# A trunk layer on one core: the second norm applied to rows ahead of the transposes, one plain half in place of three in the up projection, and the rounded blocks of w_down made inside the up projection

## The chip, the cores and the metric

The kernel runs on one core of a Trainium2 chip. The metric is the device time of one execution in microseconds (us). Matmuls run on TensorE (PE; PEld is its weight load), element work on VectorE (DVE) and ScalarE (ACT), and GpSimd (POOL) and SyncE (SP) mostly issue DMAs: SP the loads and stores, POOL those that add what they read to what lies at the destination. Each engine goes through its own instructions in the order in which they stand.

## The reference

One layer on 512 tokens of width 2048, all in float32, with a feed-forward width F of 5632:

```python
h = rms_norm(x, pre_mix_g)
# q, k, v, u from h @ w_in; chunked attention -> a; pooling of u -> p
m = concat([a, p]) @ w_o
x = x + rms_norm(m, post_mix_g)
h = rms_norm(x, pre_ffn_g)
up = causal_dwconv(h @ w_up, conv_w, conv_b)          # 3 taps along the tokens
y = (gelu(up[..., :F]) * up[..., F:]) @ w_down
x = x + rms_norm(y, post_ffn_g)
```

`rms_norm(x, g)` is x times one over the root of the row's mean square, times g per column.

## The kernel before, in words

**Numbers.** A matmul takes a float32 operand as two parts: hi, the value rounded by ACT, and lo, the rest, which DVE subtracts (`split`). A plain product sums three matmuls, hi x hi, hi x lo and lo x hi (`mm3`, L162 to L165). The products of the up projection carry the lo parts of h side by side with the hi parts in one 512-wide operand, so they take one wide matmul (L170) and one narrow one (L176) for each of 8 blocks of 128 rows (`mm2`).

**w_o.** The product with w_o is made from seven products of half size (the scheme of Strassen and Winograd) in the order 1, 2, 5, 3, 6, 7, 4, each in two column halves cc; `wo_product(i, cc)` takes four weight tiles q, and after each may call a function `between(q)`. The rows of x are in four tiles of 128 tokens: the first half is tiles 0 and 1, the second tiles 2 and 3. When y of a half is complete, its squares (L910, ACT), the norm (L952 to L955, with a power on POOL at L954), and x2 = x + y*r*gain (L967, DVE) follow. `keep_x` squares x2 for the next norm and stores x2 (L974; the second half to x2d in DRAM).

**Transposes.** `turn_back(t0, pair, ps)` transposes x2, not normed, for two blocks of 128 columns, by PE (L981), and splits the result out of PSUM with the gain of the next norm (L143 on ACT, L144 on DVE) into hT, the tiles gT0 to gT3. The eight pairs of the first half stand inside products (7,1) and (4,0); those of the second half come after w_o.

**Ready blocks.** The down projection also is made of seven products. For some of its block sums, SP's copies and POOL's adds in DRAM (`sums_in_dram`, copy L304, add L308, one step at each call of `more_sums`) make the sums t40, t41 and others. Six other parts are loaded, split and stored as hi and lo while w_o runs: `ready_blocks`, one step after each weight tile of a w_o product.

**Up projection.** F is cut in 22 blocks u of 256 columns, each with a gate (p = 0) and a value (p = 1): 44 halves. Three are plain (PLAIN = 3): 16 blocks of rows x 2 column blocks x `mm3`. The gate of u = 0 is made in two parts of 256 tokens (`gate_part`), its first part ahead of and between the transposes of the second half. The other 41 halves are made by seven products each, of sums of quarters of h (hs: h5, h3, h6, and the difference of quarters in hT) and of sums of blocks of w_up. The class `Factors` holds the order of all products (pairs (k, i): half k, product i), loads the raw blocks (SP, `raw4` and `raw_x` rings), adds the second block to them by a POOL DMA (L1362, `add`), and splits them into the `w4` ring (`make`); `prefetch(n)` keeps `make` four products and the loads ten ahead. `seven` issues a product, `keep` takes it from PSUM, `keep_all` puts a half together and multiplies it by RR. h here is not normed: R, one over the root of the mean square per token, is spread over partitions by a matmul (L223) and multiplied into every half afterwards (L1243 for plain ones).

After that follow the taps, the gelu, the product, which goes to gd in DRAM, and the down projection.

**What sets the order.** PE's order is written by hand; the other engines' rows stand as their producers and consumers are called, with `issue_after` at some places. A row's semaphore waits hold all that stands behind it on its engine.

Of the kernel before, what the change touches and what calls it, by code (L numbers as in the profile page):

```python
# [30 lines left out]
PLAIN = 3  # L31
CU = 4
AHEAD = 3
SCALE = 1.0 / math.sqrt(DH)
# [47 lines left out]
def encoder_layer(ctx: ExitStack, tc: tile.TileContext, x, xT, vecs, rel, post_mix, post_ffn,  # L82
# [427 lines left out]
    weights.limit = len(specs)  # L510
# [102 lines left out]
    with tc.tile_pool(name="p1", bufs=2, reuse_waits="tile") as p1:  # L613
# [225 lines left out]
        def ready_blocks():  # L839
            for at, j in ready_parts:  # L840
                v, hi = (p2.tile([P, 1024], dt, tag=tag, name=tag) for tag, dt in (("rw", F32), ("rwh", F32R)))
                lo = v.bitcast(F32R)
                nc.sync.dma_start(v.rearrange("p (a b) -> p a b", a=2),
                                  first_block(at[0], at[1] - 1, 0)[:, 2 * j:2 * j + 2, :])
                for _ in range(4):
                    yield
                split(hi, lo, v)
                yield
                for dest, part_ in zip(ready_w[at], (hi, lo)):
                    nc.sync.dma_start(dest[:, 2 * j:2 * j + 2, :], f32(part_).rearrange("p (a b) -> p a b", a=2))  # L850
                for _ in range(3):
                    yield

        ready_steps = ready_blocks()

# [3 lines left out]
        def wo_product(i, cc, left, between=None):  # L859
            at = 2 * cc + (4 if i in (2, 5, 3) else 0)  # L860
            ps = wo_banks[at:at + 2]
            for q in range(4):
# [6 lines left out]
                if i != 1:  # L869
                    next(ready_steps, None)  # L870
# [12 lines left out]
    with tc.tile_pool(name="p2", bufs=1, reuse_waits="tile") as p2:  # L883
        def rows2(name):

            return p2.tile([P, 2, D // 2], F32, tag=name, name=name)

        y11, y12, y21, y22 = (rows2(f"y{n}") for n in (11, 12, 21, 22))
        gain = p2.tile([P, D], F32, name="gain")
        nc.sync.dma_start(gain, post_mix[None, :].to_broadcast([P, D]))  # L890
        small = p2.tile([P, 64], F32, name="small")
        ssq = small[:, :16].rearrange("p (a b) -> p a b", a=NT)
        ssq2, rm = (small[:, i:i + 8].rearrange("p (a b) -> p a b", a=NT) for i in (16, 24))
        total = small[:, 32:36]
        nc.vector.memset(ssq, 0.0)

# [11 lines left out]
        def square(v, total):  # L908
            junk = p2.tile([P, D // 2], F32, tag="junk", name="junk")
            nc.scalar.activation(junk[:, :v.shape[-1]], v, AF.Square, accum_out=total)  # L910
# [64 lines left out]

        def turn_back(t0, pair, ps):

            for k in range(2):
                kb = 2 * pair + k
                for t in range(2):  # L980
                    nc.tensor.transpose(ps[:, k * T + t * P:k * T + (t + 1) * P],  # L981
                                        xn[t0 + t][:, kb * P:(kb + 1) * P], ident)
# [72 lines left out]
        rstd(rt, total)  # L1055

    mixing.close()

# [683 lines left out]
```

## Time and profile before

| what | us or share |
|---|---|
| runs | 1860.69, 1864.02, 1864.48 (median 1864.02) |
| profiled execution | 1858.89, span 1857.1 |
| PE busy | 1842.6 (99%) |
| DVE busy | 1532.2 (83%) |
| ACT busy | 1084.4 (58%) |
| POOL busy | 302.8 (16%) |
| mean granted clock of TensorE | 0.999 |

Busy time is the union of an engine's instructions; the rest of the span it waits. A row of the timeline gives start, length, engine, line, operation, output from input; "x8" is eight such in a row, and brackets tell how long the engine stood idle before it and what released it.

### The profile page before, as it was taken

What the parts mean: (1) busy time and instruction counts of PE and PEld (TensorE: products, weight loads), DVE (VectorE), ACT (ScalarE), POOL (GpSimd) and SP (SyncE); (2) the same over time, 40 slices, a digit from 0 to 9 for tenths busy, and PEclk for the clock granted to TensorE, in tenths of its full rate; (3) what the DMA queues carried; (4) which work ended last, traced back from release to release, by engine and by line L of the source; (5) the groups of instructions that cost most, each with busy time, mean ns of one, the idle gap of its engine ahead of it and who ended that gap; (6) DMA issues with size and microseconds to landing.
All of it is one profiled execution on the core that took longest, in us unless ns stands there. A gap on an engine that the chain in (4) does not pass through costs nothing.

```text
span 1857.1 us, 25452 instructions
## 1 busy us (share of the span) xinstructions
PE 1842.6 (99%) x9598; PEld 1584.3 (85%) x9598; DVE 1532.2 (83%) x1799; ACT 1084.4 (58%) x1376; POOL 302.8 (16%) x402
## 2 busy tenths in 40 slices
PE   9999999999999999999999999999999999999998
PEld 7888888888879888888888888888888888888886
DVE  6988778878588988888887888888887899899876
ACT  7654455456564666566565665666655655565553
POOL 3411001100000112212122122121121001111101
PEclk9999999999999999999999999999999999999999
DMA  8599977998987798888888988889888977777785
GB/s 319 171 319 302 322 230 233 267 264 310 326 308 202 185 220 195 205 204 200 201 200 203 207 202 195 204 206 205 199 179 288 363 224 171 193 211 178 176 230 157
DMA packets 139338, 426.01 MB, mean 229 GB/s; under 512 B 11920, under 2 KB 15376, under 8 KB 133520
## 3 DMA queue, kind: packets, MB, share of 16 engines
q0 software_dynamic: 54864, 173.56, 45.8%
q1 hardware_dynamic: 84352, 250.84, 38.8%
q8 instruction: 75, 1.23, 0.3%
q14 instruction: 47, 0.39, 0.1%
HBM read 370.35 MB, written 104.33 MB: 256 GB/s over the span
## 4 chain that ended last, share of the span: by engine, by line
PE 69%; DMA 1%; DVE 1%; issue 0%; ACT 0%; DVEq 0%; POOLq 0%; ACTq 0%
PE qa L170 16%; PE qa L176 8%; PE qg L170 8%; PE qg L176 4%; PE qd L170 4%; PE pa L162 4%; PE pa L165 4%; PE pa L164 4%; PE qd L176 2%; PE pg L162 2%; PE pg L165 2%; PE pg L164 2%; PE up L165 1%; PE up L162 1%; PE up L164 1%; PE pd L164 1%
## 5 line engine op out<-in xcount | busy, mean ns | idle before, releaser
L140 ACT ACTIVATE wfh<-wx 128x1024 fp32r<-128x1024 f32 x192 | 203.4, 1059 | 154.3 <-PE qg L170 54.4
L170 PE MATMUL qa<-gT,wfh 128*128 128x512 f32 x1152 | 288.6, 392 | 0.0
L141 DVE TENSOR_TENSOR wfl<-wx,wfh 128x1024 fp32r<-128x1024 f32 x192 | 234.6, 1222 | 61.0 <-ACT wfh L140 44.0
L170 PEld LDWEIGHTS qa<-gT,wfh 128*128 128x128 f32 x1152 | 207.2, 189 | 37.1
L1362 POOL DMA_DIRECT2D wx<-in_w_up x122 | 104.6, 858 | 502.6 <-DVE wfl L141 467.9
L140 ACT ACTIVATE wfh<-wy 128x1024 fp32r<-128x1024 f32 x96 | 101.7, 1060 | 108.5 <-PE qg L170 57.2
L170 PE MATMUL qg<-h,wfh 128*128 128x512 f32 x656 | 162.2, 389 | 0.1
L176 PE MATMUL qa<-gT,wfl 128*128 128x256 f32 x1152 | 161.4, 283 | 0.6 <-ACT zm L1422 0.6
L176 PEld LDWEIGHTS qa<-gT,wfl 128*128 128x128 f32 x1152 | 151.5, 191 | 4.9 <-ACT zm L1422 0.8
L170 PEld LDWEIGHTS qg<-h,wfh 128*128 128x128 f32 x656 | 122.9, 188 | 25.9 <-ACT zb L1418 0.5
L141 DVE TENSOR_TENSOR bl<-b,bh 128x2048 fp32r<-128x2048 f32 x56 | 127.2, 2285 | 19.1 <-ACT bh L140 11.7
L140 ACT ACTIVATE bh<-b 128x2048 fp32r<-128x2048 f32 x56 | 106.0, 1911 | 52.8 <-DVE b L1126 21.8
L141 DVE TENSOR_TENSOR wfl<-wy,wfh 128x1024 fp32r<-128x1024 f32 x96 | 117.1, 1220 | 12.6 <-ACT wfh L140 7.8
L162 PE MATMUL pa<-bh,ah 128*128 128x512 f32 x320 | 124.5, 389 | 0.0
L164 PE MATMUL pa<-bl,ah 128*128 128x512 f32 x320 | 124.5, 389 | 0.0
L165 PE MATMUL pa<-bh,al 128*128 128x512 f32 x320 | 124.5, 389 | 0.0
L141 DVE TENSOR_TENSOR wfl<-wz,wfh 128x1024 fp32r<-128x1024 f32 x48 | 58.7, 1223 | 54.2 <-PE qa L170 54.2
L176 PEld LDWEIGHTS qg<-h,wfl 128*128 128x128 f32 x656 | 89.5, 190 | 6.4
L170 PE MATMUL qd<-gT,wfh 128*128 128x512 f32 x384 | 94.9, 389 | 0.0
L176 PE MATMUL qg<-h,wfl 128*128 128x256 f32 x656 | 91.5, 282 | 0.0
L170 PEld LDWEIGHTS qd<-gT,wfh 128*128 128x128 f32 x384 | 71.9, 188 | 14.9
L170 PE MATMUL qa<-h,wfh 128*128 128x512 f32 x328 | 82.1, 392 | 0.0
(554 smaller groups left out, 4352.5 us busy)
## 6 DMA issues: line engine op xcount, KB each, us to landing
wx<-in_w_up POOLq DMA_DIRECT2D x122, 512.0 KB, 6.2
b<-in_w_down SPq DMA_DIRECT2D x32, 1024.0 KB, 7.0
wt<-in_w_o POOLq DMA_DIRECT2D x24, 1024.0 KB, 16.8
wx<-in_w_up SPq DMA_DIRECT2D x43, 512.0 KB, 5.5
wz<-in_w_up SPq DMA_DIRECT2D x41, 512.0 KB, 5.7
wy<-in_w_up SPq DMA_DIRECT2D x41, 512.0 KB, 4.7
wy<-in_w_up POOLq DMA_DIRECT2D x41, 512.0 KB, 6.7
sum<-part POOLq DMA_DIRECT2D x38, 512.0 KB, 6.4
```

Of the source, the lines that this page charges most:

```text
L140: rounded = nc.scalar.activation(hi, src, AF.Copy)
L141: rest = nc.vector.tensor_sub(lo, src, f32(hi))
L162: nc.tensor.matmul(ps, l[0], r[0], start=first, stop=False, skip_group_check=onto)
L164: nc.tensor.matmul(low, l[0], r[1], start=False, stop=False, skip_group_check=onto)
L165: nc.tensor.matmul(ps, l[1], r[0], start=False, stop=last, skip_group_check=onto)
L170: nc.tensor.matmul(ps, w[0][:, kb], pairs[kb][0], start=fresh and not kb, stop=last, skip_group_check=not fresh)
L176: nc.tensor.matmul(ps[:, sl], w[1][:, kb], pair[:, sl], start=False, stop=last, skip_group_check=not fresh)
L1362: nc.gpsimd.dma_start(self.raw[k, what], self.block(k, m, kh), accum_op=ALU.add)
```

## The change

h of the second half is normed as rows before it is transposed: the same factor that R brought is now multiplied into x2 ahead of the transposes (ACT for tiles 0 and 1, DVE for tiles 2 and 3). The transposes' results are kept whole in `wholes` (ACT's copy with the gain), and splits and h sums read these; the multiplications by R and RR go. The transposes of the first half all stand in product (4,0), two pairs for each weight tile. One half is plain, with its gate in full width; the others are by seven products. The products begin in another order, five of them ahead of the transposes of the second half, and their blocks are prefetched from product (4,1) of w_o on. The ready blocks leave w_o and go into the order of the products, at every 24th place from the 60th.

```diff
-PLAIN = 3
+PLAIN = 1
+READY_FROM, READY_EVERY = 60, 24
...
-        ready_steps = ready_blocks()
...
-                if i != 1:
-                    next(ready_steps, None)
...
+        def norm_x(t0):
+            r = rn[:, t0:t0 + 2]
+            nc.vector.reduce_sum(r, ssq2[:, t0:t0 + 2, :], axis=AX.X)
+            nc.vector.tensor_scalar(r, r, 1.0 / D, EPS, op0=ALU.mult, op1=ALU.add)
+            nc.gpsimd.tensor_tensor(r, r, mhalf[:, :2], op=ALU.pow)
...
         def turn_back(t0, pair, ps):
...
-                                        xn[t0 + t][:, kb * P:(kb + 1) * P], ident)
+                                        hn[t0 + t][:, kb * P:(kb + 1) * P], ident)
...
-                turn_back.last = split(*g_half(hT, kb, t0 // 2), ps[:, k * T:(k + 1) * T], col(V_PREFFN, kb))
+                nc.scalar.activation(v[:, kb % 8, :], ps[:, k * T:(k + 1) * T], AF.Copy, scale=col(V_PREFFN, kb))
+            if pair % 2:
+                i = pair // 2 % 2
+                split(*quarter(pair // 4, t0 // 2, i), v[:, 4 * i:4 * i + 4, :])
...
-        finish_last(0, wo_product(4, 0, a22, first_half(4)))
-        ps4 = wo_product(4, 1, a22)
+        finish_last(0, wo_product(4, 0, a22, first_half))
...
+                self.alone, self.open = (0, 1, 2, 3, n - 1), False
...
-                begin = [(0, 1), (0, 2), (0, 5), (1, 1), (0, 3)]
+                begin = [(k, i) for k in range(3) for i in (1, 2)] + [(0, 5), (3, 1), (0, 3), (3, 2), (0, 6)]
...
+                self.order[6:6] = [("w", q) for q in range(4)]
+                for at in range(len(ready_parts)):
+                    self.order.insert(READY_FROM + READY_EVERY * at, (None, at))
...
+                if k is None:
+                    at, j = ready_parts[i]
+                    parts = w4("rwh"), w4("rwl")
+                    split(*parts, self.raw[k, i])
+                    for dest, v in zip(ready_w[at], parts):
+                        nc.sync.dma_start(dest[:, 2 * j:2 * j + 2, :], f32(v).rearrange("p (a b) -> p a b", a=2))
...
+        ps4 = wo_product(4, 1, a22, lambda q: factors.prefetch(q + 1))
         finish_last(1, ps4)
         norm(2)
...
+        x2(2, y21, 0, whole)
+        x2(2, y22, 1, whole)
+        keep_x(2)
+        norm_x(2)
+        for t in range(2, 4):
+            hn[t] = acc8(f"hn{t}", "A")
+        for l in range(2):
+            cs = slice(l * D // 2, (l + 1) * D // 2)
+            for t in range(2, 4):
+                nc.vector.tensor_scalar_mul(hn[t][:, cs], xn[t][:, cs], rn[:, t:t + 1])
...
-            nc.vector.tensor_mul(flat(z), flat(z), flat(RR))
...
+        for k, i in factors.order[:5]:
+            start(k, i)
+        for pair in range(4):
+            turn_back(2, pair, bank(f"xt{pair}"))
+            more_sums(1)
+        start(2, 2)
+        for pair in (4, 5):
+            turn_back(2, pair, bank(f"xt{pair}"))
+        factors.open = True
+        ups = [bank(f"up0_{j}") for j in range(2)]
+        for q in range(4):
+            if q == 1:
+                for pair in (6, 7):
+                    turn_back(2, pair, bank(f"xt{pair}"))
...
+            w = weights.get(f"w00_{q}", 0)
...
+        h_sums()
+        gates[0] = gate(0, plain_z(ups))
```

In the new source most of these lines stand one or more lines further down (L308 becomes L309, L304 becomes L305, L140 and L141 become L141 and L142; L1362 becomes L1087).

POOL's queue after w_o, before: t40 and t41 are sums of w_down blocks, small holds the norm's numbers (L954 is the power of a norm), rt is R's row, and wx the first block that a product of the up projection takes as a sum.

```order
L954 TENSOR_TENSOR small_4123<-small_4123,mhalf_82 128x2 [waits DVE_49,PE_49,Activation_49]
L308 DMA t40_114<-in_w_down 512x1x512 [waits DMAHW0_49]
L954 TENSOR_TENSOR small_4123<-small_4123,mhalf_82 128x2 [waits DVE_49]
L308 DMA t41_115<-in_w_down 512x1x512 [waits DMAHW2_49]
L218 TENSOR_TENSOR rt_117<-rt_117,mhalf_82 128x4 [waits DVE_49,Activation_49]
L1362 DMA wx_5725<-in_w_up 128x1024 [waits DMAHW5_49,DMAHW4_49,DMAHW6_49,DMAHW3_49,DMAHW7_49,DMAHW1_49,DVE_49]
```

The same place after: L971 is the power of the row norm, and wx_5430 the block of product (0,5).

```order
L944 TENSOR_TENSOR small_4130<-small_4130,mhalf_82 128x2 [waits DVE_49]
L309 DMA t40_114<-in_w_down 512x1x512 [waits DMAHW2_49]
L971 TENSOR_TENSOR small_4130<-small_4130,mhalf_82 128x2 [waits DVE_49]
L309 DMA t41_115<-in_w_down 512x1x512 [waits DMAHW5_49]
L1087 DMA wx_5430<-in_w_up 128x1024 [waits DMAHW4_49,DMAHW3_49,DMAHW6_49,DMAHW1_49,DMAHW7_49,DMAHW0_49,Activation_49]
```

t40's add now stands behind the norm of y and ahead of the row norm's power, and the first block sum directly behind t41's add.

SP's queue at the same place, before: w00 to w01 are plain weights, x2d the stores of x2.

```order
L152 DMA w10_1r_5177<-in_w_up 128x2x512 [waits DMAHW1_49,DVE_49]
L304 DMA t40_114<-t60_112 16x16384 [waits DMAHW0_49,DMASW2_49]
L152 DMA w10_2r_5384<-in_w_up 128x2x512 [waits DMAHW3_49,DVE_49]
L304 DMA t41_115<-t61_113 16x16384 [waits DMAHW2_49,DMASW3_49]
L152 DMA w10_3r_5435<-in_w_up 128x2x512 [waits DMAHW4_49,DVE_49]
L152 DMA w01_0r_5486<-in_w_up 128x2x512 [waits DMAHW5_49,DVE_49]
L974 DMA x2d2_4112<-x2_5205 128x2048 [waits DVE_49]
L974 DMA x2d3_4113<-x3_5207 128x2048 [waits DMAHW6_49,DVE_49]
```

And after:

```order
L153 DMA w00_3r_5180<-in_w_up 128x2x512 [waits DMAHW4_49,DVE_49]
L305 DMA t40_114<-t60_112 16x16384 [waits DMASW2_49]
L964 DMA x2d2_4112<-x2_4968 128x2048 [waits DMAHW3_49,DVE_49]
L964 DMA x2d3_4113<-x3_5100 128x2048 [waits DVE_49]
L305 DMA t41_115<-t61_113 16x16384 [waits DMAHW5_49,DMASW3_49]
L1062 DMA wx_5430<-in_w_up 128x1024 [waits DMAHW6_49,DVE_49]
L1062 DMA wx_5433<-in_w_up 128x1024 [waits DMAHW7_49,DVE_49]
```

t41's copy moved from ahead of the x2d stores to behind them, and the load of wx_5430 is behind both.

ACT's queue where the last transposes of the second half are evacuated, before (xt30 and xt31 are the last banks of transposes):

```order
L140 ACTIVATE w10_1h_5437<-w10_1r_5177 128x1024 [waits DMAHW7_49,PE_49]
L143 ACTIVATE gT3_4809<-xt30_5443,vec_69 128x256 [waits PE_49]
L143 ACTIVATE gT3_4809<-xt31_5452,vec_69 128x256 [waits PE_49]
L143 ACTIVATE gT3_4809<-xt30_5443,vec_69 128x256 [waits DVE_49]
L143 ACTIVATE gT3_4809<-xt31_5452,vec_69 128x256 [waits DVE_49]
```

And after (a21 and a22 are `wholes` of the second half, h50 an h sum, wfh the rounded block of a product):

```order
L141 ACTIVATE gT2_4788<-a22_5220 128x4x256 [waits Activation_49]
L141 ACTIVATE wfh_5442<-wx_5430 128x1024 [waits DMASW6_49,DVE_49,PE_49]
L989 ACTIVATE a22_5220<-xt6_5471,vec_69 128x256 [waits PE_49]
L989 ACTIVATE a22_5220<-xt6_5471,vec_69 128x256
L989 ACTIVATE a22_5220<-xt7_5478,vec_69 128x256 [waits PE_49]
L989 ACTIVATE a22_5220<-xt7_5478,vec_69 128x256
L141 ACTIVATE h50_5575<-a22_5220 128x4x256 [waits DVE_49]
L141 ACTIVATE gT3_4789<-a22_5220 128x4x256 [waits Activation_49]
```

The rounding of the block that POOL's add completes (DMASW6) now stands ahead of the last evacuations; before, no block sum was read until the plain halves were through.

More of the change, by code (lines that the diff above doesn't have):

```diff
@@ L1017, in encoder_layer @@
+        factors = Factors()
+        ps4 = wo_product(4, 1, a22, lambda q: factors.prefetch(q + 1))
         finish_last(1, ps4)
         norm(2)
[L1021 to L1029 removed]
@@ L1466, in encoder_layer @@
             next(r)
-        end = factors.alone[-1]
         def next_first():
```

384 lines of the change are left out of this document (180 added, 204 removed).

## Prediction

> **What bounds the kernel now.** First the page: which engine has no idle time.
>
> ```profile
> span 1857.1 us, 25452 instructions
> PE 1842.6 (99%) x9598; PEld 1584.3 (85%) x9598; DVE 1532.2 (83%) x1799; ACT 1084.4 (58%) x1376; POOL 302.8 (16%) x402
> ```
>
> TensorE is 99% busy, so a change pays by taking matmuls away and costs wherever it makes PE wait. The next view is the same busy time by stretch (columns: stretch, length, PE, PEld, DVE, ACT, POOL, granted clock, DMA share, GB/s); the third is the list of waits from 490 to 660.
>
> ```profile
> 480.00:552.00 72.00, 69.30 (x321) 57.11 (x320) 52.94 (x62) 43.89 (x69) 0.72 (x1) 1.00 0.88 318
> 552.00:622.00 70.00, 70.00 (x420) 62.49 (x419) 59.78 (x77) 35.41 (x52) 6.76 (x6) 1.00 0.67 196
> 622.00:1400.00 778.00, 777.33 (x4464) 686.00 (x4463) 647.54 (x762) 474.95 (x581) 168.08 (x201) 1.00 0.88 202
> PEld m L164 <- DVE wo_1l L141: 3.0, 1, 3.0
> PE m L164 <- DVE wo_1l L141: 2.7, 1, 2.7
> ACT rwh L140 <- DMA rw<-in_w_down: 9.3, 2, 5.8
> ```
>
> PE never waits between 552 and 622, where the plain halves stand, nor to speak of in the up projection. It waits once before that, in w_o: 2.7 us. Two rows of the timeline show that wait and its source.
>
> ```profile
> 505.93 1.06 ACT L140 ACTIVATE rwh<-rw 128x1024 fp32r<-128x1024 f32 x1 [5.84 <-DMA rw<-in_w_down]
> 512.86 4.86 DVE L967 SCALAR_TENSOR_TENSOR x<-y,small,x 128x1024 f32<-128x1024 f32 x4
> 517.64 1.21 DVE L141 TENSOR_TENSOR wo_1l<-wo_1r,wo_1h 128x1024 fp32r<-128x1024 f32 x1
> 518.91 0.50 PE L164 MATMUL m<-wo_1l,s 128*128 128x512 f32 x1 [2.70 <-DVE wo_1l L141]
> ```
>
> ACT stood 5.84 us for a rounded block of w_down (rw); the squares behind it, the norm and x2 came late, and the rounding of wo_1 stood behind x2 on DVE.
>
> **The change part by part.** Times below count from T0, when PE leaves the last product of w_o; before it is about 551.7, by the row of ACT that was waiting for it.
>
> ```profile
> 551.68 0.60 ACT L910 ACTIVATE junk<-m 128x512 f32<-128x512 f32 x1 [0.77 <-PE m L165]
> 554.74 0.28 PE L164 MATMUL up<-gT,w_0h 128*128 128x256 f32 x1
> 562.06 0.28 PE L165 MATMUL up<-gT,w_3l 128*128 128x256 f32 x1
> 562.18 1.03 PE L981 MATMUL xt<-ident,x 128*128 128x128 f32 x8
> 605.84 0.60 PE L223 MATMUL R<-ident,rt 128*128 128x128 f32 x4
> 619.67 0.39 PE L165 MATMUL up<-gT,w_3l 128*128 128x512 f32 x1
> 622.39 0.39 PE L165 MATMUL up<-gT,w_3l 128*128 128x512 f32 x1
> 622.62 1.98 PE L170 MATMUL qa<-gT,wfh 128*128 128x512 f32 x8
> 625.39 2.00 PE L170 MATMUL qd<-gT,wfh 128*128 128x512 f32 x8
> ```
>
> *PE's work.* The step of a narrow matmul is (562.06-554.74)/61 = 0.120 us, of a wide one (622.39-619.67)/12 = 0.227, of a whole product of the seven 625.39-622.62 = 2.77. Before, three plain halves cost 192 x 0.120 (the gate in 256 columns) + 2 x 96 x 0.227 = 66.6, and spreading R another 0.4. After: one plain half, 21.8, and 14 products, 38.8. That removes 67.0-60.6 = 6.4 us of PE, which nothing hides. The transposes stay 64, 0.1 us each (8 take about 0.8).
>
> *The ready blocks leave w_o.* ACT's 5.84 us wait goes, and with it PE's wait (2.7 on PE, 3.0 on its weight loads; 2.9 taken). What is late next there: x2, the row norm and its multiplications of the first half must be done before the transposes of product (4,0). By the durations of these rows x2 ends 36 us ahead of T0 and is needed at 33 ahead; the normed rows stand at 26 ahead, needed at 22. I find no new wait. Gain: 2.9; so far -9.3.
>
> *The stretch after T0.* PE's work there is five products (13.9), 16 transposes (1.6), one product (2.8), 8 transposes (0.8), the plain half with 8 more (21.8 + 0.8), two products (5.6) and half of the wide part of (0,3) (0.9): 48.2 us until PE needs the low part of h31. Nothing in it may begin before its rows are normed, and those hang on one chain through DVE, ACT and POOL.
>
> ```profile
> 543.30 1.06 ACT L910 ACTIVATE junk<-x 128x1024 f32<-128x1024 f32 x1
> 557.77 5.38 DVE L967 SCALAR_TENSOR_TENSOR x<-y,small,x 128x512 f32<-128x512 f32 x8
> 612.79 0.43 DVE L1265 TENSOR_SCALAR RR<-RR 128x512 f32<-128x512 f32 x1
> 585.69 1.22 DVE L141 TENSOR_TENSOR w_0l<-w_0r,w_0h 128x1024 fp32r<-128x1024 f32 x1
> 591.37 1.21 DVE L141 TENSOR_TENSOR w_1l<-w_1r,w_1h 128x1024 fp32r<-128x1024 f32 x1
> ```
>
> Before, x2 begins 6.1 after T0; after, one rounding is ahead of it, so about 6.5. Four rows at 4.86 end at 11.4. ACT then squares x2 and x3 (4 x 1.06 and the reads of the sums, with two roundings of plain weights between): 15.4. Reduce, scale, the power on POOL: 16.8. The first two multiplications of a row, 0.65 each (from 0.43 for 512): the transposes can begin near 18.2. PE is there at 13.9: a **first wait** of 4.3, where before the transposes of x2 followed x2 at once and narrow matmuls covered them.
>
> DVE after that: the split of h, the sums and the weights are rows of 128x1024, one each (591.37-585.69)/5 = 1.135 us. Added up in the order of its queue, DVE has 48.3 us of rows from T0 to h31's low part, against PE's 48.2, and it has to sit out the norm (idle twice) and its start. Alone it reaches h31 at 55.6: 7.4 of stall in all. That is the floor, if ACT and the DMAs are never late.
>
> *The queue behind the block sum.* ACT's queue has wfh of product (0,5) ahead of the evacuations of xt6 and xt7, hence ahead of gT3 and the h sums. That block is a sum of two, the second added by a POOL DMA. In POOL's queue this add stands behind t40's add, the power of the norm and t41's add, and t41's add waits for t41's copy, which SP issues only after the x2d stores (before: ahead of them).
>
> ```profile
> 547.51 0.58 SPq L304 DMA_DIRECT2D t<-t  x1
> t<-t SPq DMA_DIRECT2D x1, 7.9
> t<-t SPq DMA_DIRECT2D x1, 9.7
> 555.74 1.19 POOL L308 DMA_DIRECT2D t<-in_w_down  x1 [43.00 <-DMA t<-t]
> t<-in_w_down POOLq DMA_DIRECT2D x1, 1024.0 KB, 12.6
> 559.45 1.20 POOL L308 DMA_DIRECT2D t<-in_w_down  x1 [1.78 <-DMA t<-t]
> t<-in_w_down POOLq DMA_DIRECT2D x1, 1024.0 KB, 19.6
> x2d<-x SPq DMA_DIRECT2D x2, 1024.0 KB, 10.6
> wx<-in_w_up POOLq DMA_DIRECT2D x1, 512.0 KB, 7.4
> ```
>
> (The last column is us from issue to landing.) After: t40's copy is issued at 5.8 (behind the last plain weights), lands 7.9 later, and its add goes out at 13.9. The x2d stores follow x2 at 10.3 and 11.4, t41's copy at 11.9; it lands 9.7 to 12.7 later (beside 2 MB of stores), 22 to 24.6. Then t41's add, and behind it the block's add. The second of the two adds before landed 7 us after the first though issued 3.7 after it (555.74 + 12.6 against 559.45 + 19.6 is 10.7 apart): adds go through one after another. So t41's add lands at 34.6 to 44.2, the block (half its size, 3 us) at **L** = 37.6 to 47.2. Not queued at all it would be the add's issue at 26.3 + 7.4 = 33.7. I take 42.5, near the middle of the queued bounds, since two adds and four loads share the stretch.
>
> When the block lands, ACT rounds it, evacuates xt6 and xt7, rounds gT3 and h50; gT3's low part is done at L + 6.4, which the fourth quarter of the plain half needs at 41.6. Then 17 DVE rows (16 x 1.135 and a wait of 0.7) to h31: L + 25.2, needed at 48.2. The whole **stall** after T0 is L - 23 = 19.5, the first wait included in it.
>
> Two rows show why a queue of adds doesn't simply share with the loads: from 567 to 573 both queues moved almost the same number of packets, of very different size.
>
> ```profile
> q1 hardware_dynamic: 214, 1.62, 67.2%
> q0 software_dynamic: 211, 0.43, 38.3%
> ```
>
> The adds' packets are small (0.43 MB in 211), so an add gains little from any share. The Trainium skill, "DMA: Bandwidth & Descriptors", in its section "Queues, rings and completion order", says that an engine takes turns between queues packet by packet and goes through one ring in order; by that rule a later add can't overtake t41's, which the two adds above agree with, and L could not be under the queued 37.6.
>
> *The ready blocks in the up projection.* Six blocks, each one rounding on ACT (1.06), one row on DVE (1.135), a load and two stores on SP's queue. DVE loses there the multiplication by RR per half (128x1024, 1.14) in 41 halves, so it is relieved. PE has no wait there now. The stores hold a pair of w4 for about as long as the 512 KB add took, 7.4 us, while the ring comes round every 11.1 (four products): hidden; bare, up to 2.8 each, 17 in all.
>
> **The sum.** -6.4 - 2.9 + 19.5 = +10.2 on the profiled execution, whose time is 1858.9 (span 1857.1): 1869.1. That execution is 5.1 under the median of the runs, 1864.0; so 1874 for the median. With L = 37.6 it is +5.3 (1869), with 47.2 +14.9 (1879), with 33.7 +1.4, and the DVE floor alone gives -1.9 (1862).
>
> **The rivals.**
>
> *The block lands early.* If t41's copy lands in 7.9 as t40's did, or adds overlap, L is 30 to 34 and the net between -1.9 and +1.4: 1862 to 1866, no change. For it: DMA share is 0.67 there, not full. Against: 19.6 for the second add. It decides at L = 32.3, where the stall equals the gain.
>
> *Faster.* The stall stays under 5.6 us: DVE's idle in the norm shrinks (the roundings of weights fill it, and PE is itself held back by the first wait, so that needs shift), and the block is loaded before ACT wants it. Then up to -9.3: 1855, likely 1858. For it: the stretch before had ACT at 35 of 70 us, half idle. Against: 48.3 us of DVE rows against 48.2 of PE leave nothing for a chain of norm that costs several us.
>
> *The ring of ready blocks stalls the up projection.* Each store that holds w4 longer than 11.1 us stops ACT and soon PE; at 2.8 each, +17 on whatever the stretch gives. Store latencies here are of MBs beside loads (10.6 for the x2d pair), near 11.1, so it can touch it.
>
> *The clock.* The one stretch with a lower granted clock is the end, where PE is busy 48.8 of 57 us.
>
> ```profile
> 1800.00:1857.00 57.00, 48.83 (x227) 40.74 (x225) 36.38 (x64) 18.91 (x42) 6.87 (x9) 0.96 0.62 172
> ```
>
> The stretch from 480 to 552, which holds w_o's wait, still has 1.00; a loss of 0.04 over some 20 us after each of three waits would be 2.4 us. This is within the range. The Trainium skill, "TensorE: Matmul & The Clock Gate", Part 1, has a rule that speaks against the change: an idle window of about 3.4 us halves the rate until the engine has been busy as long; by it, an estimate, each long wait would cost about 1.7 us more. No row of before holds a wait so long outside the tail.
>
> **How the numbers follow.** The queue case, 1866 to 1880, has 0.62; the ring on top of it 0.06 (1880 and more); the early block 0.17; faster 0.15. The measurement can tell about 0.2%, 3.7 us, from no change: same is 1860.3 to 1867.7. The queue case has a small part there, the early block most of its own: faster 0.15, same 0.17, slower 0.68. For 8 in 10 the range takes the floor of DVE at 1861 and the upper queue bound with the clock's share, 1881: 0.13 is left under it and 0.06 above.
>
> **What would show it.** In the profile after: PE's busy time 6 us less before the waits; no wait on rwh or wo_1l near 518; a wait of PE on transposes about 14 us after T0; ACT's wfh waiting on the add for (0,5), with xt6 behind it; PE waits on gT3 and on h31. If t41's add lands before 30 us after T0, or ACT rounds the block without waiting, the forecast's main term is wrong; if PE waits on w4 in the up projection every 24 products, the ring is the cause.

## The result and the profile after

The changed kernel takes 1896.97 us (median of runs from 1895.72 to 1899.03) against 1864.25 for the kernel before: a ratio of 1.018, with a 95% interval from 1.0162 to 1.0197. The forecast was 1874, in a range from 1861 to 1881: the sign was right, the loss was three times as large (32.7 us where 10 were forecast).

First the page of the changed kernel, then the six largest of its waits of PE (columns: us in total, times, longest).

```profile
span 1893.8 us, 25400 instructions
PE 1851.8 (98%) x9530; PEld 1586.0 (84%) x9530; DVE 1489.4 (79%) x1782; ACT 1105.6 (58%) x1449; POOL 310.1 (16%) x411
```

```profile
PE qg L171 <- ACT m L1410: 9.1, 6, 3.8
PE qa L177 <- ACT m L1415: 7.6, 5, 2.9
PE up L163 <- ACT gT L141: 6.7, 1, 6.7
PE xt L984 <- DVE hn L1150: 2.9, 2, 2.6
PE qa L177 <- ACT m L1419: 2.8, 2, 1.8
PE pd L165 <- DMA bl<-rw02l: 2.5, 1, 2.5
```

These six add up to 31.6 us. PE's busy time rose by 9.2 though 6.4 us of matmuls went: the remaining ones ran 15.6 us longer. Where that is, the timeline of PE tells, with ACT's and POOL's rows that belong to it. T0 is 548.2 here (552.1 before, where the last matmul of w_o starts at 551.9).

```profile
548.16 1.98 PE L171 MATMUL qa<-gT,wfh 128*128 128x512 f32 x8
564.84 0.33 PE L984 MATMUL xt<-ident,hn 128*128 128x128 f32 x1 [2.58 <-DVE hn L1150]
596.63 0.79 PE L163 MATMUL up<-gT,w_3h 128*128 128x512 f32 x1 [6.71 <-ACT gT L141]
606.00 1.98 PE L171 MATMUL qg<-h,wfh 128*128 128x512 f32 x8
607.81 1.11 PE L177 MATMUL qg<-h,wfl 128*128 128x256 f32 x8
615.55 3.78 PE L171 MATMUL qg<-h,wfh 128*128 128x512 f32 x8 [3.83 <-ACT m L1410]
619.12 1.81 PE L177 MATMUL qg<-h,wfl 128*128 128x256 f32 x8
663.86 1.22 PE L177 MATMUL qa<-gT,wfl 128*128 128x256 f32 x8 [2.92 <-ACT m L1415]
664.92 3.50 PE L171 MATMUL qa<-gT,wfh 128*128 128x512 f32 x8
971.89 3.50 PE L171 MATMUL qg<-h,wfh 128*128 128x512 f32 x8 [2.39 <-ACT m L1410]
```

```profile
592.17 1.06 ACT L141 ACTIVATE wfh<-wx 128x1024 fp32r<-128x1024 f32 x1 [16.75 <-DMA wx<-in_w_up]
892.55 1.06 ACT L141 ACTIVATE wfh<-wz 128x1024 fp32r<-128x1024 f32 x1 [2.98 <-DMA rw11l<-rwl]
```

The first of ACT's rows is the forecast's main term: ACT stands 16.75 us for the block of (0,5), and rounds it 44.0 us after T0 (42.5 was forecast). PE's wait on gT3 (596.63) is behind it, and (0,3), at 615.55, starts 67.4 after T0 where PE's own work would have let it start at 47.3 (the forecast's 48.2 less half of the wide part of (0,3)): a stall of 20.1, against 19.5 forecast. POOL's rows and the DMA issues (last column: us from issue to landing) show the queue.

```profile
569.59 1.19 POOL L309 DMA_DIRECT2D t<-in_w_down  x1 [5.59 <-DMA t<-t]
573.72 0.91 POOL L1087 DMA_DIRECT2D wx<-in_w_up  x1 [2.94 <-ACT a L989]
t<-in_w_down POOLq DMA_DIRECT2D x1, 1024.0 KB, 17.8
t<-in_w_down POOLq DMA_DIRECT2D x1, 1024.0 KB, 20.1
wx<-in_w_up POOLq DMA_DIRECT2D x1, 512.0 KB, 18.4
```

t40's add, issued at 562.06, lands at 562.1 + 17.8 = 579.9, t41's at 569.6 + 20.1 = 589.7, and the block's, issued 4.1 us after t41's, at 573.7 + 18.4 = 592.1: 2.4 us behind it.

What the forecast didn't have starts there. From 615 to 670 stand six more waits of 0.2 to 2.92 us (8.1 in all), and the matmuls behind the wait of 3.83 and behind the longest of the six ran at about half rate: eight wide ones took 3.78 and 3.50 us where 1.98 is usual. Between 800 and 1100 stand five waits of 0.97 to 2.39 (7.3 in all), one for each of five of the six ready blocks. The table puts the difference of the two spans together, from the starts of groups of matmuls.

| stretch | before | after | difference |
|---|---|---|---|
| start to T0 | 552.1 | 548.2 | -3.9 |
| T0 to the first matmul of the down projection (1423.3; 1456.2) | 871.2 | 908.1 | +36.9 |
| from there to the end | 433.8 | 437.6 | +3.8 |
| span | 1857.1 | 1893.8 | +36.7 |

In the middle stretch 6.4 us of PE's work went, so 43.3 came: 20.1 up to (0,3), 12.1 from 615 to 670 (8.1 of waits, 4 of half rate, from 3.57 and 1.65 against 1.81 and 0.95 for (0,3), and 3.30 against 1.84 at 664.9), 8.8 at the ready blocks (7.3, and 1.5 of half rate at 971.9). 2.3 remain spread. Of the 3.8 in the last stretch 1.9 is PE's wait on rw02l (2.45, where the kernel before has 0.6 for the same operand); the rest was not followed up, and no run was made for either.

### The profile page after: what moved, and what is told of

Read it like the earlier page. It is cut to its first block, busy times and chain, and to the rows that moved or that the text cites. A ratio compares the mean times of both kernels' runs of the same rounds, so it can differ in the third digit from the quotient of the medians.

```text
span 1893.8 us, 25400 instructions
## 1 busy us (share of the span) xinstructions
PE 1851.8 (98%) x9530; PEld 1586.0 (84%) x9530; DVE 1489.4 (79%) x1782; ACT 1105.6 (58%) x1449; POOL 310.1 (16%) x411
## 4 chain that ended last, share of the span: by engine, by line
PE 87%; DMA 6%; DVE 3%; issue 2%; ACT 1%; POOL 0%; SPq 0%; POOLq 0%; DVEq 0%; ACTq 0%
PE qa L171 16%; PE qa L177 9%; PE qg L171 8%; PE qg L177 4%; PE qd L171 4%; PE pa L163 4%; PE pa L165 4%; PE pa L166 4%; PE m L163 3%; PE m L166 3%; PE m L165 3%; PE qd L177 2%; PE pg L163 2%; PE pg L165 2%; PE pg L166 2%
## 5 line engine op out<-in xcount | busy, mean ns | idle before, releaser
L171 PE MATMUL qa<-gT,wfh 128*128 128x512 f32 x1200 | 302.1, 394 | 0.0
L142 DVE TENSOR_TENSOR wfl<-x,wfh 128x1024 fp32r<-128x1024 f32 x165 | 202.0, 1224 | 91.6 <-ACT wfh L141 83.4
L171 PEld LDWEIGHTS qa<-gT,wfh 128*128 128x128 f32 x1200 | 216.7, 190 | 39.0
L141 ACT ACTIVATE wfh<-x 128x1024 fp32r<-128x1024 f32 x165 | 174.4, 1057 | 111.0 <-PE qg L171 44.3
L1087 POOL DMA_DIRECT2D x<-in_w_up x125 | 107.5, 860 | 489.6 <-DVE wfl L142 459.8
L171 PE MATMUL qg<-h,wfh 128*128 128x512 f32 x688 | 174.1, 396 | 9.1 <-ACT m L1410 9.1
L177 PE MATMUL qa<-gT,wfl 128*128 128x256 f32 x1200 | 168.5, 283 | 10.3 <-ACT m L1415 7.6
L177 PEld LDWEIGHTS qa<-gT,wfl 128*128 128x128 f32 x1200 | 157.8, 191 | 16.6 <-ACT m L1415 9.2
L171 PEld LDWEIGHTS qg<-h,wfh 128*128 128x128 f32 x688 | 130.6, 191 | 38.9 <-ACT m L1410 11.9
L142 DVE TENSOR_TENSOR bl<-b,bh 128x2048 fp32r<-128x2048 f32 x56 | 127.2, 2287 | 18.6 <-ACT bh L141 11.7
L141 ACT ACTIVATE wfh<-wy 128x1024 fp32r<-128x1024 f32 x100 | 105.3, 1053 | 60.8 <-PE qd L171 39.9
L141 ACT ACTIVATE bh<-b 128x2048 fp32r<-128x2048 f32 x56 | 106.1, 1914 | 55.9 <-DVE b L1217 23.3
L142 DVE TENSOR_TENSOR wfl<-wy,wfh 128x1024 fp32r<-128x1024 f32 x100 | 121.9, 1219 | 13.5 <-ACT wfh L141 9.2
L177 PEld LDWEIGHTS qg<-h,wfl 128*128 128x128 f32 x688 | 95.0, 193 | 6.9
L171 PEld LDWEIGHTS qd<-gT,wfh 128*128 128x128 f32 x400 | 75.3, 189 | 15.4
L142 DVE TENSOR_TENSOR wfl<-wz,wfh 128x1024 fp32r<-128x1024 f32 x50 | 61.2, 1223 | 28.4 <-PE qa L171 22.4
```

The lines of the kernel that those rows point to most:

```text
L141: rounded = nc.scalar.activation(hi, src, AF.Copy)
L142: rest = nc.vector.tensor_sub(lo, src, f32(hi))
L171: nc.tensor.matmul(ps, w[0][:, kb], pairs[kb][0], start=fresh and not kb, stop=last, skip_group_check=not fresh)
L177: nc.tensor.matmul(ps[:, sl], w[1][:, kb], pair[:, sl], start=False, stop=last, skip_group_check=not fresh)
L1087: nc.gpsimd.dma_start(self.raw[k, what], self.block(k, m, kh), accum_op=ALU.add)
```

## The experiments

Theory: the stall up to (0,3) is the queue of adds ahead of one block, handed on by ACT's queue; the waits behind it and those of the ready blocks have causes of their own. Rivals stand in the expectations. Ratios are to the kernel before in the same job, and where runs of different jobs are compared, the ratios are; the changed kernel's is 1.0180. Times after T0 are from each run's own T0, 548.4 to 549.5 in the runs below for which they are given. Lines left out of an edit are marked by "...".

### The sums moved late (late), the rounding moved back (act), and both

```diff
 # late
-            more_sums(1)                      # 4 steps, at the transposes of pairs 0 to 3
...
+            if i == 4 and k in (29, 30, 31, 32):
+                with tc.issue_after(factors.last):   # the last load on SP
+                    more_sums(1)
 # act: in the plain half, at q = 1
...
+                    for ins in (split.last, split.rest):   # the split of gT3
+                        behind.enter_context(tc.issue_after(ins))
...
-            factors.prefetch(factors.AHEAD)
+                factors.prefetch(factors.AHEAD - (q == 0))
```

> The four steps that make t40 and t41 (two copies, two adds) are taken out of the stretch after w_o and put at the ends of halves 29 to 32 of the up projection; nothing else changes. Theory of the queue: with no other add ahead of it the block sum of product (0,5) is issued as in the changed kernel (25.6 us after T0) and lands some 8 to 10 us later, so ACT rounds it near 34 us after T0 and not at 44.0; product (0,3) then starts near 57 to 58 after T0 and not at 67.4. About 1887 us (10 less than the changed kernel). If the waits behind h31 (about 12 us from 615 to 670) also come from that crowd of transfers, they shrink too: 1878 to 1882. Rival, that the DMA engines are simply full of loads and stores there: the block lands at 40 or later and the time stays at 1893 to 1897.

> Only the place of the rounding of the (0,5) block changes: on ACT and on DVE it is queued behind the evacuation of the last transposes and the split of gT3. The block lands when it did (about 44 after T0). Theory that ACT's queue hands the late block on to everything behind it: PE's wait for gT3 (6.7 + 0.7) goes; (0,5) itself can start near 47 and h31 is late by DVE's rows alone, so (0,3) starts near 56 to 58 and not at 67.4: about 1886 us. Rival, that the block itself is what PE needs and the queue only shows it first: the wait moves to product (0,5) and the time stays within 1893 to 1898.

> Both edits at once. Theory: what is left after T0 is the norm's wait at the transposes (2.9) and DVE's own rows, with h31 near 55.6 and (0,3) near 56: about 1885 us if the waits behind h31 stay, 1875 to 1880 if they come from the crowd of transfers. Rival, that both edits take the same wait away: no more than the better of the two alone.

late: 1903.01, 1.0225 (1.0202 to 1.0249). act: 1891.87, 1.0176 (1.0147 to 1.0204). Both: 1902.77, 1.0223 (1.0202 to 1.0245). Rows of ACT and PE of late:

```profile
578.18 1.06 ACT L141 ACTIVATE wfh<-wx 128x1024 fp32r<-128x1024 f32 x1 [2.53 <-PE up L165]
601.75 2.36 PE L171 MATMUL qg<-h,wfh 128*128 128x512 f32 x8 [0.61 <-DVE zc L1298]
1202.55 2.07 PE L177 MATMUL qa<-gT,wfl 128*128 128x256 f32 x8 [5.04 <-ACT m L1415]
```

The queue's part came out: ACT rounds the block of (0,5) 29.4 us after T0 and waits there for PE, no longer for a DMA, and (0,3) starts at 53.0. The time rose all the same: where the sums now stand PE waits 5.04, 0.73 and 3.54 us, and the ready blocks' longest wait grew from 2.39 to 4.35. The sums' two copies and two adds of 1 MB cost more in the up projection than at w_o's end. So late tells where the block's delay is from, and its total tells nothing of it. Rows of act:

```profile
592.42 1.06 ACT L141 ACTIVATE wfh<-wx 128x1024 fp32r<-128x1024 f32 x1 [9.04 <-DMA wx<-in_w_up]
601.61 2.07 PE L171 MATMUL qg<-h,wfh 128*128 128x512 f32 x4 [4.55 <-DVE h L142]
612.10 2.08 PE L171 MATMUL qg<-h,wfh 128*128 128x512 f32 x8 [3.09 <-DVE h L142]
```

The wait on gT3 is gone, but the block landed as late as ever, with the h sums behind it on ACT, and PE waited for these instead: (0,3) starts 62.6 after T0, 4.8 us earlier, and the time can't be told from that of the changed kernel. The rival was nearer.

### The sums moved early (early, early_act)

```diff
-            more_sums(1)                      # at the transposes of pairs 0 to 3
+                if i == 6 and q % 2:          # in wo_product, 4 times
+                    more_sums(1)
```

> The four steps of t40 and t41 go into the products (6,0) and (6,1) of w_o, about 60 us ahead of T0, where the DMA share of the changed kernel is 0.72. Theory of the queue: the (0,5) block is rounded near 36 us after T0 (36.3 where the sums stood late) and not at 44.0, and there is no price for the sums elsewhere, so the time falls by what product (0,3) starts earlier, 7 to 9 us: 1888 to 1890. Rival, that the sums have to be paid wherever they stand: a new wait of PE in w_o, or L unchanged, and 1895 to 1900.

> Sums in w_o, and the rounding of the (0,5) block behind the split of gT3. If what the two edits take away is one wait, this gives no more than the early sums alone, 1887 to 1890, with DVE's rows setting h31; if the block's place on ACT counts even where it lands at 36, it is 3 to 5 us less than that.

early: 1883.59, 1.0120 (1.0105 to 1.0135). early_act: 1881.65, 1.0118 (1.0098 to 1.0139). Rows of early, the issue of its block's add, and a stretch from issue to landing of that add in early, then in the changed kernel (columns of the last two as in the prediction's stretches):

```profile
577.03 1.06 ACT L141 ACTIVATE wfh<-wx 128x1024 fp32r<-128x1024 f32 x1 [2.42 <-PE up L165]
600.60 2.35 PE L171 MATMUL qg<-h,wfh 128*128 128x512 f32 x8 [0.61 <-DVE zc L1300]
wx<-in_w_up POOLq DMA_DIRECT2D x1, 512.0 KB, 5.9
566.94:572.84 5.90, 5.77 (x35) 4.89 (x35) 5.90 (x11) 5.90 (x13) 1.80 (x2) 1.00 1.04 322
573.72:592.12 18.40, 16.19 (x76) 13.15 (x74) 4.85 (x6) 1.67 (x3) 1.78 (x2) 1.00 1.06 263
```

The block of (0,5) is rounded 28.4 us after T0, with no wait for a DMA (the 36.3 that the expectation takes from late is the rounding of the next block, that of (3,1)), and (0,3) starts at 52.0, 15.4 us earlier. No wait was added in w_o. By the ratios the time fell by 11 us of these 15; the waits at the ready blocks grew from 7.3 to 9.0, and the rest was not followed up. So the main term is shown: two adds that nobody needs before the down projection, with their copies, stood ahead of a block that PE needed within 50 us. That the DMA engines are simply full there, the rival of late, is out: their share is as high in early while the block's add is under way (1.04; 1.06 in the changed kernel), and the add lands 5.9 us after its issue in place of 18.4. It is also issued sooner, 18.3 after T0 in place of 25.6; what the copies and the adds each give there, early doesn't tell, since it moves both. With that gone, the rounding's place on ACT is worth nothing that can be told.

### The ready blocks: copies, inplace, own, phase, own_phase

copies and inplace leave out the rounding of each block: two copies from DRAM to DRAM put the raw block in the place of both parts, so no tile of the w4 ring and no row of ACT or DVE is used; in inplace the copies are tied behind a load on SP. own takes other tiles, phase other places.

```diff
 # own
-                    parts = w4("rwh"), w4("rwl")
+                    parts = RR.rearrange("p a b -> p (a b)").bitcast(F32R), self.raw[k, i].bitcast(F32R)
 # phase
-READY_FROM, READY_EVERY = 60, 24
+READY_FROM, READY_EVERY = 56, 28
...
 # copies (inplace: under tc.issue_after(self.last))
+                    for dest in ready_w[at]:
+                        nc.sync.dma_start(dest[:, 2 * j:2 * j + 2, :],
+                                          first_block(at[0], at[1] - 1, 0)[:, 2 * j:2 * j + 2, :])
```

> The six ready blocks of the up projection are replaced by copies of the raw blocks from DRAM to DRAM (one to the place of hi, one to that of lo), so the values of the down projection are wrong, but the stores' bytes stay; no tile of the w4 or raw rings, no rounding on ACT and no row on DVE is used for them. Theory of the ring: the five waits of PE between 810 and 1100 (0.97, 1.35, 2.39, 1.24, 1.35, and about 1.5 of half clock behind the third) go: 1888 us. Rival, that the waits come from the traffic of the blocks: they stay, 1896 to 1898.

copies: 1895.14, 1.0181 (1.0158 to 1.0204). No wait is left between 800 and 1110, but the copies depend on nothing and were issued from 38.6 us after the start on: PE's busy time in the first 100 us fell from 98.5 to 93.7, with a wait of 4.2 for a norm there, and the first matmul behind w_o starts at 559.8 in place of 548.2. The run says that the blocks are the cause of the five waits, not which part of them.

> As the run with copies, but each pair of copies is now queued on SP behind the load that stood ahead of the ready block, so that its bytes (half a megabyte read and written twice) move in the up projection at the same six places; no tile, no rounding and no DVE row is used, and the down projection's values are wrong. Theory of the ring: PE doesn't wait between 800 and 1110, and the time is 1886 to 1889. Rival, traffic: waits of about 1 to 2 us stay at the six places, 1894 to 1898.

inplace: 1887.67, 1.0147 (1.0130 to 1.0164). One wait of 0.90 is left where there were five. That looked like the ring; but the rounding, its DVE row and one of three transfers of each block had gone with it.

> The changed kernel with its six ready blocks complete, but the rounded part goes to the tile that held R and RR (unused here) and the rest takes the place of the raw block, so that no pair of the w4 ring waits for the stores; loads, rounding, DVE row and stores stay as they are. Theory of the ring: the five waits of PE between 800 and 1110 go, as in the run with the copies in place (1887.7): 1886 to 1890. Rival, that what goes with the copies is ACT's and DVE's work or the third half-megabyte: waits stay and the time is above 1893.

own: 1898.73, 1.0189 (1.0167 to 1.0211), a miss: the ring was freed and the time didn't fall. Three waits (2.80, 5.01 and 1.52) took the place of five. The rows are PE's and ACT's, SP's and POOL's at the first of them, and the DMA issues.

```profile
736.74 2.11 PE L171 MATMUL qg<-h,wfh 128*128 128x512 f32 x8 [2.80 <-ACT m L1410]
735.39 0.81 ACT L1297 ACTIVATE zc<-zc,vec 128x512 f32<-128x512 f32 x1 [4.11 <-DMA gd<-zc]
724.65 0.43 SPq L1099 DMA_DIRECT2D rw01h<-RR  x1
726.56 0.33 SPq L1099 DMA_DIRECT2D rw01l<-rw  x1
725.10 1.49 POOL L1341 DMA_DIRECT2D gd<-zc  x2 [2.54 <-DVE zc L1338]
rw01h<-RR SPq DMA_DIRECT2D x1, 512.0 KB, 8.5
gd<-zc POOLq DMA_DIRECT2D x2, 256.0 KB, 9.1
```

The block's two stores are issued within 2 us of the store of the finished gate and value (gd), which then needs 9.1 us where the median between 686 and 1110 is 4.8; the next gate's taps write the same tile, so ACT waits for it, and PE for ACT. ACT waits for gd at the other two as well (6.26 and 2.83); at the longest the block's stores were issued 5 to 6 us ahead of gd's.

> The changed kernel with the ready blocks at every 28th place from the 56th (the same place of every fourth half) and not at every 24th from the 60th; the w4 ring holds them as before. If the ring is what PE waits for, its waits between 780 and 1110 stay at 1 to 2.4 us each, 1895 to 1898. If what counts is the meeting with the store of gd, and this place avoids it, they go: 1886 to 1890. If the traffic itself costs: 1894 to 1898, with waits at other places.

> The same places with the ring freed (rounded part in the tile of R and RR, rest in place). If the meeting with the gd store is what remains without the ring, no wait of PE is left between 700 and 1110, and the time is 1886 to 1890. If the traffic of the blocks costs wherever it stands, three or more waits of 1.5 to 5 us stay and it is 1895 to 1899.

phase: 1893.95, 1.0156 (1.0133 to 1.0179). own_phase: 1887.20, 1.0123 (1.0102 to 1.0145). With the place alone the waits at the blocks stay (0.85, 1.53, 2.44, 0.27, 0.85, 1.53); with place and ring together none is left between 700 and 1110, and by the ratios the time is 10.6 us lower. Either cause alone is covered by the other, and the price of the six blocks, 8.8 by the timeline, is both together: tiles of the w4 ring held until their stores land, and stores at a place where they meet other transfers. In own that is gd's store. In the changed kernel ACT waits by name for ready blocks' stores at the third block (the row at 892.55) and the sixth (1.81 and 1.82), but ahead of the longest of PE's five waits, the 2.39, it stands for an add and then 1.09 for gd:

```profile
968.40 1.06 ACT L141 ACTIVATE wfh<-x 128x1024 fp32r<-128x1024 f32 x1 [3.82 <-DMA x<-in_w_up]
```

How much of the place is gd and how much the adds, the runs don't tell apart.

### Ahead and together: early_own, early_own_act, eight, best

```diff
 # eight, beside early and own
...
-                begin = [(k, i) for k in range(3) for i in (1, 2)] + [(0, 5), (3, 1), (0, 3), (3, 2), (0, 6)]
+                begin = [(k, i) for k in range(4) for i in (1, 2)] + [(0, 5), (0, 3), (0, 6)]
...
-        for k, i in factors.order[:5]:
+        for k, i in factors.order[:8]:
...
```

> Sums of t40 and t41 in w_o and ready blocks without the w4 ring. The two prices stand at different places, so the two gains (13.4 and, if the ring is right, about 9) add up: 1873 to 1876. Rival, that PE's late start only fills what the ring then costs anyway: 1880 to 1883.

> As before it, and the rounding of the (0,5) block is queued behind the split of gT3. With the block landing at 36 us its place on ACT is worth little: within 3 us of the run with the sums in w_o and the ring freed.

> Sums in w_o, ring freed, and all eight products that need only the first half of h ((0,1) to (3,2)) stand ahead of the transposes, as cover for the norm of the second half: PE has 22.2 us of work where the normed rows are ready at about 18 to 20. Theory: the wait at the transposes (2.2 + 0.3, and about 1 to 2 of half clock) goes, while the end of the stretch has 5.5 us less work of PE ahead of h31, so part comes back there: 1 to 4 us less than without it, 1870 to 1874. Rival, that DVE's rows alone set h31 whatever PE does ahead of it: no gain, and a longer wait at (0,3).

> All four edits: sums of t40 and t41 in w_o, the (0,5) rounding behind the split of gT3, ring freed, blocks at every 28th place. If the places are right: 1871 to 1876 (1883.0 less the waits of 2.33, 4.08, 0.78 and about 2 of half clock). If the traffic costs anywhere: 1881 to 1885.

early_own: 1883.51, 1.0110 (1.0086 to 1.0134); early_own_act: 1883.04, 1.0105 (1.0084 to 1.0125); eight: 1884.52, 1.0119 (1.0096 to 1.0142). The first was a miss, for the reason that own showed. In eight PE has more work ahead of the transposes, and waits on DVE all the same.

```profile
573.16 1.50 PE L986 MATMUL xt<-ident,hn 128*128 128x128 f32 x12 [1.41 <-DVE first_parts L1409]
605.45 3.78 PE L171 MATMUL qg<-h,wfh 128*128 128x512 f32 x8 [3.40 <-DVE zc L1300]
```

(0,3) starts 57.1 after T0, 5.1 later than in early, and behind a longer wait: no gain, as the rival of this run had it. But DVE's rows don't set h31 alone: ACT's first evacuation of the transposes is 5.4 later too (23.0 after T0 in place of 17.6), and h31 moved with the transposes.

best: 1871.51, 1.0046 (1.0030 to 1.0062), within its forecast. By the ratios, 25 of the 33 us go with four edits together: sums in w_o, rounding behind the split, ring freed, blocks at another place. Rows of best:

```profile
565.29 0.33 PE L986 MATMUL xt<-ident,hn 128*128 128x128 f32 x1 [2.20 <-DVE hn L1152]
602.10 2.08 PE L171 MATMUL qg<-h,wfh 128*128 128x512 f32 x8 [1.75 <-DVE h L142]
613.46 1.22 PE L177 MATMUL qa<-gT,wfl 128*128 128x256 f32 x8 [2.73 <-ACT m L1417]
650.01 2.08 PE L177 MATMUL qa<-gT,wfl 128*128 128x256 f32 x8 [2.92 <-ACT m L1417]
```

### The waits behind h31: noadd, best_noadd, fill

noadd and best_noadd leave out the adds that follow a rounding in halves 0 to 3, so products 6, 7 and 4 of these use blocks that lack a term.

```diff
 # noadd
+                if k < 4:
+                    pass
-                if i == 1 and k not in self.alone:
+                elif i == 1 and k not in self.alone:
 # fill, beside best
-                ... [(0, 5), (3, 1), (0, 3), (3, 2), (0, 6)]
+                ... [(0, 5), (3, 1), (0, 3), (0, 6), (3, 2)]
```

> The POOL adds that follow a rounding (made for products 5, 6 and 3) are left out in halves 0 to 3, so their products 6, 7 and 4 use blocks that lack a term; the first add for product 5 stays. Theory: the waits of PE behind h31 (1.37, 1.80, 0.21, 0.69, 1.14, 2.92 and the half clock after two of them, about 12 us between 615 and 670) come from adds that bunch up after the stall, with 9 to 11 us from issue to landing; without them ACT never waits for a DMA there and they go: 1885 to 1888. Rival, that ACT and DVE are behind with the h sums, the gate's taps and the roundings: the waits stay, 1894 to 1898.

> best without the adds that follow the roundings in halves 0 to 3 (wrong blocks for their products 6, 7 and 4). Theory: the waits behind h31 (2.38, 0.65, 0.69, 3.66 and about 2 of half clock in the run with the early sums, the freed ring and the later rounding) come from adds that have no other products between them, since products 1 and 2 of halves 1 to 3 were taken ahead; without adds at most the 0.69 stays: 6 to 9 us less than best. Rival, DVE and ACT behind: within 3 us of best.

> best with product (3,2) between (0,6) and (0,7) instead of ahead of (0,6). If the add between 6 and 7 lacks cover, the first wait behind h31 (2.73 on the block of (0,7)) goes or falls under 1, the later ones (2.17, 0.69, 1.62, 2.92) stay, and the time is 1868 to 1870. If the adds are late for another reason (they pass through one queue at their own rate), nothing changes: 1870 to 1873.

noadd: 1891.13, 1.0162 (1.0137 to 1.0187), a smaller gain than expected: the six waits of 8.1 became three of 3.5, while the one at (0,3) grew from 3.83 to 4.67 and that on gT3 from 6.7 to 8.0. best_noadd: 1863.63, 1.0009 (0.9993 to 1.0024), 7.9 below best: the waits of 2.73, 2.17, 0.69, 1.62 and 2.92 became 0.69, 0.69 and 1.80. fill: 1871.72, 1.0059 (1.0047 to 1.0071), no gain: the wait of 2.73 went, and one of 4.18 came two to three products later. The longest wait left behind h31 in best_noadd, and that of fill:

```profile
642.95 1.22 PE L177 MATMUL qa<-gT,wfl 128*128 128x256 f32 x8 [1.80 <-ACT m L1419]
620.44 2.08 PE L177 MATMUL qa<-gT,wfl 128*128 128x256 f32 x8 [4.18 <-ACT m L1421]
```

So most of the wait behind h31 is for adds: without them 3.2 us of 10.1 remain. That two products stand next to each other isn't their cause. In the changed kernel three adds were issued from 619.8 to 622.9, and they took 5.4, 8.6 and 10.9 us, where the median of the 125 of the last one's kind is 6.5. Why they crowd there, and whether the order of the first halves could prevent it, stays open.

### Before, with the ready blocks' wait shortened (before_rw)

```diff
-                for _ in range(4):
+                for _ in range(6):
                     yield
                 split(hi, lo, v)
...
-                for _ in range(3):
-                    yield
+                yield
```

> The kernel before, with six steps in place of four between the load of a ready block and its rounding (and one in place of three behind its stores), so that ACT doesn't stand 5.84 us for the block ahead of product (7,1). By the prediction's term PE's wait of 2.7 to 3.0 on wo_1l goes: 1858 to 1860, a ratio of 0.998 to 0.999. Rival, that ACT then only stands at another place: no change within 1 us.

before_rw: 1861.05, 1.0002 (0.9990 to 1.0013). ACT's wait for the block only went from 5.84 to 5.35 and PE's from 2.7 to 2.2, since the load itself goes out only 0.8 us earlier: the edit didn't do what it was made for, and the term was not tested by it. That T0 comes 3.9 us earlier in the changed kernel, with no wait on wo_1l, speaks for it, and doesn't show it.

## Why the prediction was wrong, point by point

- **PE's work, -6.4.** Right by its steps: at full rate a product takes 2.8 from start to start in the changed kernel too, as the sum has it. PE's busy time doesn't show it bare: in best and best_noadd it is 1840.1 and 1840.5 against 1842.6 before, 2.5 and 2.1 less, and the mean granted clock 0.998 and 0.997 against 0.999; that the lower rate behind the remaining waits is the whole rest is not shown.
- **Ready blocks out of w_o, -2.9.** T0 came 3.9 earlier, and PE's idle time ahead of it fell from 4.95 to 1.50; 2.7 of this is the wait on wo_1l, which is gone. Right in kind, 1 us too small; that the ready blocks alone are the cause is not shown.
- **The stall up to h31, L - 23 = 19.5 with L = 42.5.** Right: L was 44.0, the stall to (0,3) 20.1, and the run with the sums in w_o took 15 us of it away by moving them alone. The queue of adds was within its bounds, t41's add at 41.5 after T0. Two sizes in it were off without harm: the two adds of the kernel before land 10.7 us apart, where the working says 7 (7 is what the second took longer from issue to landing), and the first wait was 2.6 and 0.3, not 4.3.
- **DVE's floor.** (0,3) would start at 54.7 by the forecast (55.6 for h31, less four wide matmuls); it started at 52.0 in early. 2.7 too high.
- **"The whole stall after T0 is L - 23."** This is the step that failed first. It ended the sum at h31 and asked of the stretch behind it nothing at all. There stood 12.1 us: waits for adds of the first halves, which crowd when DVE and ACT come back from the h sums, and matmuls at half rate. The forecast had asked what is late next for the wait in w_o, but not here.
- **"Hidden; bare, up to 2.8 each, 17 in all."** The step on the ready blocks failed second: 8.8 us. The working compared 7.4 us of a store with a ring of 11.1. The twelve stores were no slower than that, 2.6 to 6.8 from issue to landing. What it had wrong is the hold and the ring's turn: the third block was rounded at 882.56 and its second store landed at 892.5, a hold of 10, and ACT stood for its tile from 889.6 on, 7.0 after the rounding. Other transfers at the same place, gd's store among them, are not in the sum at all. The rival that names the ring had about twice the price, 17, and too small a chance, 0.06; and it named part of the cause.
- **The clock.** The forecast allowed 2.4 us. The granted clock by stretch was (columns as before):

```profile
592.00:600.00 8.00, 2.71 (x6) 1.82 (x7) 5.57 (x5) 7.10 (x10) 1.75 (x2) 0.59 0.52 83
600.00:605.00 5.00, 5.00 (x16) 3.97 (x15) 5.00 (x6) 2.39 (x4) 0.00 (x0) 0.64 0.77 194
605.00:610.00 5.00, 5.00 (x28) 4.28 (x27) 5.00 (x5) 3.91 (x5) 0.86 (x1) 1.00 0.18 22
```

PE was 15.6 us longer on less work. 6.0 of it lies inside the stall (53.3 busy for 47.3 of work), where a slower PE costs little: DVE goes without a gap from 595.7 to (0,3). 4 us behind h31 and 1.5 at the ready blocks are on the path.
- **The range.** It took in bounds of the queue and left the ring at 0.06 and the stretch behind h31 out. The three terms (20.1, 12.1, 8.8) are not exclusive cases, but they were priced as if they were: the likeliest is their sum.

## What to carry to other kernels

Where a wait goes to the place at which a buffer chain starts, follow the chain on for as long as it needs to come back into step; the sum doesn't end when the first late operand arrives. A background DMA is priced by what it meets: ask for each queue what is issued within the next 10 us and who waits for that, and expect causes that cover each other, so that removing one alone can show nothing. A sum that nobody needs for 800 us should not stand ahead of one that is needed in 50.

## What the runs showed of the hardware that was not expected

The rate of PE can halve after waits shorter than the longest one that the kernel before has. In the changed kernel eight wide matmuls took 3.78 us after a wait of 3.83, 3.50 after 2.92, and 3.50 after 2.39; they took about 2 after waits of 1.80 and less. In noadd a wait of 1.86 was enough:

```profile
765.97 3.67 PE L171 MATMUL qg<-h,wfh 128*128 128x512 f32 x8 [1.86 <-ACT m L1412]
```

But in w_o of the kernel before, a wait of 2.70 was followed by matmuls of the usual step, and in act one of 3.09 (the row at 612.10) by eight in 2.08. So the length of a wait alone doesn't decide. The Trainium skill, "TensorE: Matmul & The Clock Gate", Part 1, tells of a free-running window of about 3.4 us: the rate falls after an idle window, and it rises after a busy one. The wait of 1.86 is much shorter than that figure, so here the measurement decides: a wait of 1.9 us can be enough, and one of 3.1 need not be.

A transfer that depends on nothing can run hundreds of us ahead of its place in the text: the twelve copies of copies, written into the up projection, were issued from 38.6 us on, where the loads that they replace go out between 718 and 1039.
